# A planner that prices the SBUF port shared by VectorE and GpSimd, and rope additions with an operand in PSUM

## The chip, the core and the metric

One core of a Trainium2 chip runs the whole program. The metric is the device time of one execution in microseconds; the time of a kernel is the median of its runs.

Five engines work side by side, each through its own instructions in their written order: TensorE (PE, matrix products, weight loads shown apart as PEld), VectorE (DVE), ScalarE (ACT), GpSimd (POOL), and SyncE (SP), which issues most DMAs. They meet through semaphores.

## The reference: two layers of a hybrid decoder

The inputs are a prompt of 512 tokens and 8 samples of 4 tokens with a past of 2048. Each of two layers computes

```
h = rmsnorm(x) * norm_w;  z = h @ w_in          # 1024 -> 3584 columns
rq, rk, rv, rg, mq, mk, mv, mg, pu, pg = split(z)
rq = rope(heads(rq)); rk = rope(heads(rk)) / 8
mq = rope(rmsnorm(heads(mq), q_norm_w)); mk = rope(rmsnorm(heads(mk), k_norm_w))
mix = concat(retention(rq, rk, rv) * silu(rg),
             block_sparse_attention(mq, mk, mv) * silu(mg),
             causal_pooling(pu) * silu(pg))
x = x + mix @ w_out
```

with 6 heads of 64 in retention and in attention. The rope of a head of 64 is `x * C + swap(x) * S`, where C and S hold cosines and sines, with the norm weights multiplied in for mq and mk, and swap exchanges the halves of 32. The samples attend to a paged cache of 2048 keys, of which the best three blocks of 256 and the own tokens count. Outputs are x, the new keys and values, and the states of retention and pooling. All of it is in float32.

## The kernel before

**Dense products.** Tokens are tiles of 128 (t = 0 to 3 of the prompt; t = 4 is the 32 sample rows). A weight chunk of 384 or 256 columns comes as four slices (`wraw`, in layer 0's first chunk `pk`). A slice is split into a rounded high part, cast by ACT, and a low part `whl = wraw - high`, a subtraction that DVE or POOL does (`low`, in `split_weights`). The activations are split in the same way into `XT`. Three passes of PE over the high and low parts then stand for one float32 product. The accumulators are two PSUM banks, `acc`: a prompt tile takes 8 x 3 = 24 matmuls of PE, and the bank is free again when the last reader of the tile is done with it.

**What follows a product.** `projected` (L616) does the rope of the q and k tiles. It multiplies the accumulator by C into an SBUF buffer `t1`, the swapped halves by S into a second one `t2` (both shown as `t`), and frees `acc`. For mq and mk it sums the squares, which ACT wrote, into `qst`; POOL takes the power -1/2 of them in `rsq`; and DVE adds `t1 + t2` and multiplies by the result into `qk` (the sample keys into `ks`). For rq and rk nothing comes from POOL, and the addition may go to DVE or POOL. PE then transposes the tile (`tr<-cst,qk`). `post_gate` multiplies a silu gate `t` into `mix` (DVE or POOL), and `split_mix` splits `mix` into `XT` (the low part on DVE or POOL). `norm_tokens` at the start squares x (ACT or POOL) and adds the squares up (DVE or POOL) in `qT` and `kT`. `pool` sums the pooling windows on POOL alone (`tabs`, `s`).

**Who goes where, and in what order.** Nothing of this order is written by hand. The code is a set of generators that yield what they want next: an engine (`R("DVE")`) or a choice of engines (`R("DVE|POOL")`), flags to wait for, buffers to take. `_Plan.run` keeps a clock for each engine and starts the task that can start first; the time that it adds for each instruction is the estimate in `_Timed`'s `call`. `_Plan._start` picks the engine of a choice: the one whose start is earliest, where POOL's start counts 0.7 us later than it is. Instructions are emitted in the planned order, so this clock settles the order on each engine; what happens on the chip is then governed by semaphores.

Dense products have the lowest priority on PE. The 16 units of sample attention in each layer (`dec`, `pv`) fill in, as their pages (`pk`, `pv_`) land.

Of the kernel before, what the change touches and what calls it, by code (L numbers as in the profile page):

```python
# [24 lines left out]
H = 6  # L25
# [92 lines left out]
class _Plan:  # L118
# [7 lines left out]
    HOLD = 0.6  # L126
    SWITCH = 0.1

    def __init__(self):
        self.mode = FULL  # L130
        self.fill = False
        self.free = {e: 0.0 for e in ("PE", "ACT", "DVE", "POOL", "SP")}
        self.dma_free = 0.0
        self.done = {}
        self.res = {k: [0.0] * n for k, n in RES.items()}
        self.tasks = []
        self.seq = 0
        self.now = 0.0
        self.engine = None
        self.stage = 0  # L140
        self.dur = 0.0
        self.late = []

    def spawn(self, gen, prio=5, at=None):
        self.seq += 1
# [34 lines left out]
    def _start(self, t):  # L180
        engines, keys, get, mode = t["want"]
        at = t["ready"]
        if engines == t.get("engine"):
            at -= self.HOP[engines]
        for k in keys:
            if k not in self.done:
                return None
            at = max(at, self.done[k])
        for name in set(get):
            n = get.count(name)  # L190
            r = self.res[name]
            if len(r) < n:
                return None
            at = max(at, sorted(r)[n - 1])
        best = None
        for e in engines.split("|"):
            s = max(at, self.free[e])
            if e == "SP":
                s = max(s, self.dma_free - 3.0)
            c = s + (0.7 if e == "POOL" and "|" in engines else 0.0)  # L200
            if e == "PE" and t["prio"][0] < 9:
                late = self.MARGIN
                if mode != self.mode:
                    late = self.HOLD if self.mode == FULL else 0.3
                c = max(at + late, self.free[e])
            if best is None or c < best[0]:
                best = (c, s, e)
        c, s, e = best
        return c if e == "PE" else s, s, e
# [33 lines left out]
def R(engines, keys=(), get=(), mode=FULL):  # L243
    return engines, tuple(keys), tuple(get), mode


class _Timed:
# [10 lines left out]
    def __getattr__(self, op):  # L258
        f = getattr(self.eng, op)

        def call(*args, **kw):
            aps = [x for x in list(args) + list(kw.values()) if hasattr(x, "free_size")]
            n = max(x.free_size() for x in aps)
            psum = any(x.space == PSUM for x in aps)
            if self.name == "DVE":
                points = sum(1 for x in args[2:] if hasattr(x, "free_size"))
                fast = op in ("tensor_copy", "tensor_scalar", "memset") and not psum
                us = ((n / 2 if fast else n) + 66) / 960.0 + 0.065 * points
            elif self.name == "ACT":
                more = sum(1 for k in ("bias", "scale", "accum_out") if hasattr(kw.get(k), "free_size"))  # L270
                more += op == "mul"
                us = n / 1200.0 + (0.05 if psum else 0.093) + 0.093 * more
            elif op == "memset":
                us = 0.03 + n * 0.00085
            elif kw.get("op") == OP.pow:
                us = 0.3 + n * 0.165
            else:
                us = 0.153 + n * 0.0021

            spans = [self._span(x) for x in aps]  # L280
            if self.last and self.last[0] == self.plan.stage and any(
                    t == self.last[1] and lo <= self.last[3] and self.last[2] <= hi for t, lo, hi in spans):
                us += 0.127
            out = kw["out"] if "out" in kw else args[0]
            self.last = (self.plan.stage,) + self._span(out)
            self.plan.use(self.name, us)
            return f(*args, **kw)  # L287

        return call
# [3 lines left out]
def trunk(ctx, tc, depth, xp, xt, xs, xst, kv, sret, spool, pt, nrow, ncol, lpar, w384, w256, cst, y0,  # L293
# [14 lines left out]
    def buf(tag):  # L308

        if tag == "whl":  # L310
            return sb([128, 2, 768], tag, RES[tag], dt=F32R)
        if tag in ("vst", "kst", "oPT"):
            return sb([96, SHAPES[tag]], tag, RES[tag], dt=F32R)
        return sb([128, SHAPES[tag]], tag, RES[tag])
# [50 lines left out]
    def heads(x):  # L365
        return x.rearrange("p (h e) -> p h e", h=H)
# [249 lines left out]
    def projected(a, dst, t, Ct, St, scale=None, eps=None, norm=None):  # L616


        rows = 128 if t < 4 else NS
        src = a[:, :384]  # L620
        if t == 4:
            yield from join_sample(a, dst[:NS], 384, norm)
            src = dst[:NS]
        s3, d3 = heads(src), heads(dst[:rows])
        if scale is None:
            if t == 4:
                yield R("ACT", (), ["t1"])
                sq = buf("t1")
                A.activation(heads(sq[:rows]), s3, AF.Square)
            else:  # L630
                yield R("ACT")
                sq = dst
                A.activation(d3, s3, AF.Square)
        yield R("DVE", (), ["t1", "t2"])
        t1, t2 = heads(buf("t1")[:rows]), heads(buf("t2")[:rows])
        V.tensor_tensor(out=t1, in0=s3, in1=Ct[:rows][:, None, :].to_broadcast([rows, H, HD]), op=OP.mult)
        sa = St[:rows, 0:32][:, None, :].to_broadcast([rows, H, 32])
        sb_ = St[:rows, 32:64][:, None, :].to_broadcast([rows, H, 32])
        V.tensor_tensor(out=t2[:, :, 0:32], in0=s3[:, :, 32:64], in1=sa, op=OP.mult)
        V.tensor_tensor(out=t2[:, :, 32:64], in0=s3[:, :, 0:32], in1=sb_, op=OP.mult)  # L640
        if t < 4:
            X.put("acc")
        if scale is None:
            st = sb([128, 2, 8], "qst", 2)
            V.tensor_reduce(out=st[:rows, 0, :H], in_=heads(sq[:rows]), axis=AX, op=OP.add)
            if t == 4:
                X.put("t1")
            yield R("POOL")
            rsq(st[:rows, 1, :H], st[:rows, 0, :H], H, rows, 1.0 / HD, EPS if eps is None else eps)
            scale = st[:rows, 1, :H]  # L650
            yield R("DVE")
            V.tensor_tensor(out=t1, in0=t1, in1=t2, op=OP.add)
        else:
            yield R("DVE|POOL")
            add2(d3 if scale is False else t1, t1, t2, OP.add)
            if scale is not False:
                yield R("DVE")
        if scale is not False:
            V.tensor_tensor(out=d3, in0=t1, in1=scale[:, :, None].to_broadcast([rows, H, HD]), op=OP.mult)
        X.put("t1")  # L660
        X.put("t2")

    def stacked(src, dst, low):

# [1206 lines left out]
```

## Time and profile before

| | us |
|---|---|
| median of 3 runs (lowest, highest) | 710.14 (709.77, 712.19) |
| the profiled execution: its time | 708.43 |
| its span, first to last instruction | 706.3 |

| engine | busy us | share |
|---|---|---|
| PE | 680.0 | 96% |
| DVE | 491.5 | 70% |
| ACT | 331.4 | 47% |
| POOL | 147.4 | 21% |

Matmuls overlap, and their ends are modelled, so PE's 96% is not a measure of how well it is used. What counts is where PE stood idle, and for whom. A row such as `PE tr L335 <- DVE qk` says that PE's transposes waited for a DVE instruction that writes `qk`. Almost every vector instruction is recorded on one line (L287, the helper that calls it), so its tiles name it: `whl<-wraw,whl` is the low part of a weight slice. A duration in a timeline row is that of all its instructions together, from the first start to the last end.

### The profile page before, as it was taken

Reading aid. Unit: us, or ns where it says so; the run is one execution under the profiler, and the core shown is the slowest. Engines: PE = TensorE matmul, PEld = TensorE weight load, DVE = VectorE, ACT = ScalarE, POOL = GpSimd, SP = SyncE. Lnnn points to the kernel's source line nnn. Section 1 sums busy time; section 2 is a strip of 40 time slices with the busy share of each in tenths; the row PEclk is TensorE's granted clock in tenths of the full one; section 3 lists DMA queues with packets and bytes.
Section 4 is the critical chain, followed back from the end, with each engine's and each line's share of the span. In section 5 each row is a group of like instructions: output and inputs, shape, how many; then the busy total and the mean of one; then the engine's idle time right before and its main releaser. Section 6 shows DMA issues by size and latency. Waiting matters only on the chain.

```text
span 706.3 us, 16977 instructions
## 1 busy us (share of the span) xinstructions
PE 680.0 (96%) x5940; PEld 572.4 (81%) x5940; DVE 491.5 (70%) x1130; ACT 331.4 (47%) x839; POOL 147.4 (21%) x165
## 2 busy tenths in 40 slices
PE   6999999999999999989999999999999999999998
PEld 4887777778878878889989767777787778889898
DVE  6868898788655469876385588986855546887632
ACT  6444667654322415355264336766624233347511
POOL 7333332200101004321141223330100010045000
PEclk9999999999999999999999999999999999999999
DMA  8467889696899894406655679899999987110552
GB/s 318 179 224 248 290 266 316 213 331 216 252 304 322 255 326 160 130 12 205 225 148 168 209 247 325 281 317 287 288 336 295 319 286 224 38 62 3 168 177 78
DMA packets 111366, 159.76 MB, mean 226 GB/s; under 512 B 13937, under 2 KB 96114, under 8 KB 111282
## 3 DMA queue, kind: packets, MB, share of 16 engines
q1 hardware_dynamic: 111010, 158.43, 68.7%
q8 instruction: 47, 0.77, 0.4%
q10 hardware_dynamic: 272, 0.26, 0.1%
q14 instruction: 37, 0.30, 0.1%
HBM read 148.80 MB, written 9.84 MB: 225 GB/s over the span
## 4 chain that ended last, share of the span: by engine, by line
PE 79%; DVE 12%; ACT 2%; issue 2%; DMA 2%; POOL 1%; SPq 1%; DVEq 0%; POOLq 0%; ACTq 0%
PE acc L325 50%; PE dec L325 10%; PE pv L325 10%; PE tr L335 6%; PE att L325 3%; DVE whl L287 2%; DVE qk L287 2%; DVE t L287 1%; DVE XT L287 1%; DMA wraw<-w 1%; DMA mix<-xt 1%; DVE mix L287 1%; SPq L1638 1%; ACT whl L287 1%; DVE pt L287 1%
## 5 line engine op out<-in xcount | busy, mean ns | idle before, releaser
L325 PE MATMUL acc<-whl,XT 128*128 128x384 f32 (+1 forms) x1680 | 313.2, 339 | 8.2 <-ACT whl L287 3.0
L325 PEld LDWEIGHTS acc<-whl,XT 128*128 128x128 f32 x1680 | 282.6, 190 | 26.1 <-issue 12.5
L325 PE MATMUL acc<-XT,whl 128*128 128x256 f32 (+1 forms) x960 | 139.5, 296 | 1.0 <-DVE t L287 1.0
L325 PEld LDWEIGHTS acc<-XT,whl 128*128 128x128 f32 x960 | 125.0, 190 | 8.8 <-issue 6.3
L287 ACT CAST whl<-wraw 128x768 fp32r<-128x768 f32 (+1 forms) x100 | 76.9, 781 | 40.7 <-PE acc L325 30.2
L287 DVE TENSOR_TENSOR whl<-wraw,whl 128x768 fp32r<-128x768 f32 (+1 forms) x79 | 74.1, 947 | 28.8 <-ACT whl L287 27.5
L287 POOL TENSOR_TENSOR whl<-wraw,whl 128x768 fp32r<-128x768 f32 (+1 forms) x21 | 36.8, 1752 | 123.3 <-ACT whl L287 123.3
L325 PE MATMUL dec<-pk,qblk 128*32 128x256 f32 x768 | 50.3, 383 | 0.9 <-PE acc L325 0.6
L325 PEld LDWEIGHTS dec<-pk,qblk 128*32 128x32 f32 x768 | 24.1, 109 | 18.5 <-issue 5.8
L287 DVE TENSOR_TENSOR pv<-pv,cst 128x384 f32<-128x384 f32 x40 | 22.5, 563 | 19.5 <-PE pv L325 19.2
L287 ACT ACTIVATE dP<-dec,stat 128x256 f32<-128x256 f32 x32 | 15.2, 474 | 36.4 <-DVE stat L287 36.2
L287 ACT ACTIVATE P<-att,ast 128x128 f32<-128x128 f32 (+3 forms) x48 | 25.2, 530 | 10.7 <-DVE ast L287 8.8
L287 POOL TENSOR_TENSOR mix<-mix,t 128x256 f32<-128x256 f32 x8 | 6.4, 799 | 110.7 <-DVE t L287 83.8
L287 DVE TENSOR_TENSOR mix<-acc,qk 128x384 f32<-128x384 f32 (+1 forms) x24 | 12.2, 509 | 22.5 <-PE acc L325 22.1
L287 POOL TENSOR_TENSOR qst<-qst,mhalf 128x6 f32<-128x6 f32 (+1 forms) x20 | 26.7, 1336 | 1.7
L287 DVE TENSOR_TENSOR t<-acc,cst 128x192 f32<-128x192 f32 (+1 forms) x48 | 17.3, 417 | 10.9 <-PE acc L325 10.8
L287 ACT COPY PT<-tr 128x128 f32<-128x128 f32 (+3 forms) x41 | 16.4, 422 | 17.3 <-PE tr L335 17.2
L287 ACT ACTIVATE t<-acc 128x256 f32<-128x256 f32 (+1 forms) x32 | 12.6, 394 | 22.0 <-DVE acc L287 11.2
L287 DVE TENSOR_REDUCE stat<-dec 128x1 f32<-128x256 f32 x32 | 13.4, 419 | 13.4 <-PE dec L325 13.2
L287 ACT ACTIVATE dPT<-dec 128x256 f32<-128x256 f32 x32 | 12.2, 381 | 21.1 <-PE pv L325 21.1
L335 PE MATMUL tr<-cst,qk 128*128 128x128 f32 (+1 forms) x108 | 18.0, 275 | 3.8 <-DVE qk L287 3.6
L335 PE MATMUL tr<-cst,P 128*128 128x128 f32 x120 | 20.0, 281 | 1.5 <-DVE P L287 0.7
(503 smaller groups left out, 1211.6 us busy)
## 6 DMA issues: line engine op xcount, KB each, us to landing
pk<-kv SPq DMA_DIRECT2D x256, 192.0 KB, 3.9
wraw<-w SPq DMA_DIRECT2D x76, 384.0 KB, 4.6
wraw<-w SPq DMA_DIRECT2D x24, 256.0 KB, 4.1
y<-mix SPq DMA_DIRECT2D x4, 512.0 KB, 3.5
mix<-xt SPq DMA_DIRECT2D x7, 256.0 KB, 6.3
pk<-w SPq DMA_DIRECT2D x4, 384.0 KB, 5.1
o_vp<-tv SPq DMA_DIRECT2D x8, 192.0 KB, 1.9
o_kp<-qk SPq DMA_DIRECT2D x8, 192.0 KB, 4.3
```

Of the source, the lines that this page charges most:

```text
L287: return f(*args, **kw)
L325: nc.tensor.matmul(out, lhsT, rhs, start=start, stop=stop)
L335: nc.tensor.transpose(out, in_, ident[:n, :n])
L1638: S.dma_start(mix[:, 2 * kp:2 * kp + 2, 256 * h:256 * h + 256], col3_(xt[h, kp]))
```

## The change

Three things change.

1. The planner's clock knows of a port. A DVE instruction of 64 or more columns without an operand in PSUM, and with two tensors or a form that runs at double rate, may not overlap with a POOL instruction of 64 or more columns other than a power. Whichever is planned second gets the remaining time of the other added to its own.
2. Where DVE and POOL may be chosen, POOL counts as starting 3.0 us later (`POOL_LAST`), not 0.7.
3. In `projected` the product with C is written back in place, into the accumulator (for t = 4 into SBUF, as its source is there). The addition reads the accumulator and `t2`, always runs on DVE, and stands right behind the sum of squares. The accumulator is freed after the addition, not before it. The power on POOL is a task of its own, and only the last multiplication waits for it. The buffer `t1` is no longer used for it.

```diff
+    POOL_LAST = 3.0
...
-            c = s + (0.7 if e == "POOL" and "|" in engines else 0.0)
+            c = s + (self.POOL_LAST if e == "POOL" and "|" in engines else 0.0)
...
+            t = self.plan.now + self.plan.dur
+            port = self.plan.port
+            if self.name == "DVE" and not psum and n >= 64 and (
+                    points >= 2 or fast or op in ("tensor_tensor", "scalar_tensor_tensor")):
+                lo, hi = port["POOL"]
+                if lo < t + us and hi > t:
+                    us += hi - max(lo, t)
+                port["DVE"] = t + us
+            elif self.name == "POOL" and kw.get("op") != OP.pow and n >= 64:
+                if port["DVE"] > t:
+                    us += port["DVE"] - t
+                port["POOL"] = t, t + us
...
-        V.tensor_tensor(out=t1, in0=s3, in1=Ct[:rows][:, None, :].to_broadcast([rows, H, HD]), op=OP.mult)
...
         V.tensor_tensor(out=t2[:, :, 32:64], in0=s3[:, :, 0:32], in1=sb_, op=OP.mult)
-        if t < 4:
-            X.put("acc")
+
+        V.tensor_tensor(out=s3, in0=s3, in1=Ct[:rows][:, None, :].to_broadcast([rows, H, HD]), op=OP.mult)
         if scale is None:
...
-            yield R("POOL")
-            rsq(st[:rows, 1, :H], st[:rows, 0, :H], H, rows, 1.0 / HD, EPS if eps is None else eps)
+            key = ("qn", X.stage)
+
+            def root():
+                yield R("POOL")
+                rsq(st[:rows, 1, :H], st[:rows, 0, :H], H, rows, 1.0 / HD, EPS if eps is None else eps)
+                X.flag(*key)
+
+            X.spawn(root(), 1, X.then())
             scale = st[:rows, 1, :H]
-            yield R("DVE")
-            V.tensor_tensor(out=t1, in0=t1, in1=t2, op=OP.add)
+            V.tensor_tensor(out=d3, in0=s3, in1=t2, op=OP.add)
+            if t < 4:
+                X.put("acc")
+            X.put("t2")
+            yield R("DVE", [key])
         else:
-            yield R("DVE|POOL")
-            add2(d3 if scale is False else t1, t1, t2, OP.add)
...
+            V.tensor_tensor(out=d3, in0=s3, in1=t2, op=OP.add)
+            if t < 4:
+                X.put("acc")
+            X.put("t2")
         if scale is not False:
-            V.tensor_tensor(out=d3, in0=t1, in1=scale[:, :, None].to_broadcast([rows, H, HD]), op=OP.mult)
+            V.tensor_tensor(out=d3, in0=d3, in1=scale[:, :, None].to_broadcast([rows, H, HD]), op=OP.mult)
```

What it does to the instructions, counted over the whole order: POOL has 41 wide instructions that the planner could have put elsewhere before, and 12 now. The weight slices on POOL go from 21 to 9, the gates from 8 to 0, the parts of `XT` from 7 to 2, the sums of the first norm from 4 to 1, the rope additions from 1 to 0. The 12 window sums stay. DVE takes 12 weight slices, 8 gates, 5 parts of `XT` and one sum of the norm more; ACT takes two squares of the norm. PE runs the same matmuls in another interleaving.

At the start, POOL's first wide instructions before are the squares of x (`qT<-mix`), sums of them (`qT<-qT`) and a weight slice; `rs` is the norm itself:

```order
L287 TENSOR_TENSOR qT<-mix 128x1024 x2
L287 TENSOR_TENSOR qT<-qT 128x1024
L287 TENSOR_TENSOR qT<-qT 128x512
L287 TENSOR_TENSOR whl<-wraw,whl 128x768
L287 TENSOR_TENSOR rs<-rs,mhalf 128x2
```

and now:

```order
L304 TENSOR_TENSOR qT<-qT 128x1024
L304 TENSOR_TENSOR whl<-wraw,whl 128x768
L304 TENSOR_TENSOR rs<-rs,mhalf 128x1
L304 TENSOR_SCALAR rs<-rs 128x1
L304 TENSOR_TENSOR rs<-rs,mhalf 128x2
```

The two squares and one sum have left POOL.

On DVE, one prompt tile of mk in layer 0 before, from the rope's products to the multiplication by the power (`qst`); `pv`, `att` and their results are other tasks' work between:

```order
L287 TENSOR_TENSOR t_1188<-acc,tabs 128x384
L287 TENSOR_TENSOR t_1189<-acc,tabs 128x6x32 x2
L287 TENSOR_REDUCE qst<-qk 128x6
L287 COPY kTs<-tr 128x96
L287 TENSOR_TENSOR pv<-pv,cst 128x384
L287 TENSOR_REDUCE On<-pv 128x64
L287 TENSOR_TENSOR att<-att,cst 128x2x128
L287 TENSOR_REDUCE ast<-att 128x2
L287 TENSOR_TENSOR t_1188<-t_1188,t_1189 128x384
L287 TENSOR_TENSOR qk<-t_1188,qst 128x384
```

and a tile of the same chunk now:

```order
L304 TENSOR_TENSOR t_1049<-acc,tabs 128x6x32 x2
L304 TENSOR_TENSOR acc<-acc,tabs 128x384
L304 TENSOR_REDUCE qst<-qk 128x6
L304 TENSOR_TENSOR qk<-acc,t_1049 128x384
L304 TENSOR_TENSOR pv<-pv,cst 128x384
L304 TENSOR_REDUCE On<-pv 128x64
L304 TENSOR_TENSOR klz<-tr,kT 64x3x128 x2
L304 TENSOR_TENSOR qk<-qk,qst 128x384
```

The addition, which reads `acc` now, stands right behind the sum of squares. Before it stood behind the other tasks' work, and `acc` was free before them, after the products.

On POOL, between the powers of the mk tiles of layer 0 (`qst`) and the weight slices of the next chunk, before:

```order
L287 TENSOR_SCALAR qst<-qst,rs 32x6
L287 TENSOR_TENSOR qst<-qst,mhalf 32x6
L287 TENSOR_TENSOR whl<-wraw,whl 128x512 x2
L287 TENSOR_SCALAR qst<-qst,rs 128x6
L287 TENSOR_TENSOR qst<-qst,mhalf 128x6
L287 TENSOR_TENSOR whl<-wraw,whl 128x512
```

and now:

```order
L304 TENSOR_SCALAR qst<-qst,rs 32x6
L304 TENSOR_TENSOR qst<-qst,mhalf 32x6
L304 TENSOR_SCALAR qst<-qst,rs 128x6
L304 TENSOR_TENSOR qst<-qst,mhalf 128x6
L304 TENSOR_SCALAR qst<-qst,rs 128x6
L304 TENSOR_TENSOR qst<-qst,mhalf 128x6
L304 TENSOR_TENSOR whl<-wraw,whl 128x512
```

Two of the three slices have gone to DVE.

## Rows read from the trace of the kernel before

**Rows 1.** The page: span, and busy time of each engine (share of span, instructions).

```profile
span 706.3 us, 16977 instructions
PE 680.0 (96%) x5940; PEld 572.4 (81%) x5940; DVE 491.5 (70%) x1130; ACT 331.4 (47%) x839; POOL 147.4 (21%) x165
```

**Rows 2.** The page: share of the span on the chain that ended last.

```profile
PE 79%; DVE 12%; ACT 2%; issue 2%; DMA 2%; POOL 1%; SPq 1%; DVEq 0%; POOLq 0%; ACTq 0%
```

**Rows 3.** Waits of PE: line, released by, total us, times, longest.

```profile
PE tr L335 <- DVE qk L287: 3.6, 4, 1.2
...
PE acc L325 <- DVE XT L287: 2.3, 1, 2.3
...
PE acc L325 <- DVE mix L287: 2.1, 1, 2.1
...
PE dec L325 <- DVE mixs L287: 1.1, 1, 1.1
...
PE acc L325 <- DVE t L287: 1.0, 1, 1.0
```

**Rows 4.** Timeline, layer 1, last key tile: start, us, engine, instruction [idle before].

```profile
620.38 0.55 DVE L287 TENSOR_TENSOR t<-t,t 128x384 f32<-128x384 f32 x1
...
620.96 1.81 POOL L287 TENSOR_TENSOR whl<-wraw,whl 128x768 fp32r<-128x768 f32 x1
...
620.97 2.21 DVE L287 TENSOR_TENSOR qk<-t,cst 128x384 f32<-128x384 f32 x1
...
623.24 0.55 PE L335 MATMUL tr<-cst,qk 128*128 128x128 f32 x3 [1.24 <-DVE qk L287]
```

**Rows 5.** Timeline, layer 0, VectorE and GpSimd side by side.

```profile
54.62 1.09 DVE L287 TENSOR_TENSOR t<-acc,tabs 128x384 f32<-128x384 f32 x3
...
54.79 1.84 POOL L287 TENSOR_TENSOR whl<-wraw,whl 128x768 fp32r<-128x768 f32 x1 [5.61 <-ACT whl L287]
```

**Rows 6.** Timeline, layer 0: a GpSimd power beside VectorE adds.

```profile
295.35 1.33 POOL L287 TENSOR_TENSOR gst<-gst,mhalf 128x6 f32<-128x6 f32 x1
...
295.67 1.01 DVE L287 TENSOR_TENSOR XT<-mix,XT 128x384 fp32r<-128x384 f32 x2
```

**Rows 7.** Groups by form: PE, VectorE, GpSimd: xcount | busy us, mean ns | idle before.

```profile
L325 PE MATMUL acc<-whl,XT 128*128 128x384 f32 x1488 | 289.7, 346 | 8.2 <-ACT whl L287 3.0 <-DVE XT L287 2.3 <-DVE mix L287 2.1
...
L287 DVE TENSOR_TENSOR whl<-wraw,whl 128x768 fp32r<-128x768 f32 x60 | 61.1, 1030 | 21.8 <-ACT whl L287 20.5 <-DMA wraw<-w 0.4
...
L287 DVE TENSOR_TENSOR mix<-mix,t 128x256 f32<-128x256 f32 x24 | 12.0, 500 | 0.5
...
L287 DVE TENSOR_TENSOR t<-t,t 128x384 f32<-128x384 f32 x23 | 13.7, 594 | 0.3
...
L287 DVE TENSOR_TENSOR t<-acc,cst 128x384 f32<-128x384 f32 x16 | 8.9, 556 | 10.9 <-PE acc L325 10.8
...
L287 DVE TENSOR_REDUCE qst<-qk 128x6 f32<-128x384 f32 x16 | 8.7, 542 | 0.0
...
L287 POOL TENSOR_TENSOR whl<-wraw,whl 128x768 fp32r<-128x768 f32 x16 | 30.4, 1900 | 120.6 <-ACT whl L287 120.6
...
L287 POOL TENSOR_TENSOR qst<-qst,mhalf 128x6 f32<-128x6 f32 x16 | 21.4, 1340 | 1.3
```

**Rows 8.** Timeline of the start: GpSimd sums, VectorE, PE.

```profile
11.16 5.73 DVE L287 TENSOR_TENSOR whl<-pk,whl 128x768 fp32r<-128x768 f32 x2
...
13.07 4.94 POOL L287 TENSOR_TENSOR qT<-qT 128x1024 f32<-128x1024 f32 x2
...
16.81 1.87 DVE L287 SCALAR_TENSOR_TENSOR XT<-mix,ncol,XT 128x256 fp32r<-128x256 f32 x2
...
18.34 0.97 PE L325 MATMUL acc<-whl,XT 128*128 128x384 f32 x4 [2.30 <-DVE XT L287]
```

**Rows 9.** Waits of PE's weight loads, same columns as rows 3.

```profile
PEld acc L325 <- DVE t L287: 2.5, 6, 1.2
```

**Rows 10.** Windows: stretch, us; busy us (count) of PE, PEld, DVE, ACT, POOL; PEclk, DMA, GB/s.

```profile
40.00:100.00 60.00, 58.10 (x480) 48.01 (x478) 50.32 (x109) 31.56 (x86) 20.56 (x22) 0.97 0.80 255
```

More of the change, by code (lines that the diff above doesn't have):

```diff
@@ L142, in __init__ @@
         self.late = []
+        self.port = {"DVE": 0.0, "POOL": (0.0, 0.0)}
     def spawn(self, gen, prio=5, at=None):
@@ L633, in projected @@
                 A.activation(d3, s3, AF.Square)
-        yield R("DVE", (), ["t1", "t2"])
-        t1, t2 = heads(buf("t1")[:rows]), heads(buf("t2")[:rows])
-        V.tensor_tensor(out=t1, in0=s3, in1=Ct[:rows][:, None, :].to_broadcast([rows, H, HD]), op=OP.mult)
+        yield R("DVE", (), ["t2"])
+        t2 = heads(buf("t2")[:rows])
         sa = St[:rows, 0:32][:, None, :].to_broadcast([rows, H, 32])
@@ L647, in projected @@
                 X.put("t1")
-            yield R("POOL")
-            rsq(st[:rows, 1, :H], st[:rows, 0, :H], H, rows, 1.0 / HD, EPS if eps is None else eps)
-            scale = st[:rows, 1, :H]
-            yield R("DVE")
-            V.tensor_tensor(out=t1, in0=t1, in1=t2, op=OP.add)
-        else:
-            yield R("DVE|POOL")
-            add2(d3 if scale is False else t1, t1, t2, OP.add)
-            if scale is not False:
-                yield R("DVE")
+            key = ("qn", X.stage)
[4 more added lines that the diff above has]
+            X.spawn(root(), 1, X.then())
+            scale = st[:rows, 1, :H]
+            V.tensor_tensor(out=d3, in0=s3, in1=t2, op=OP.add)
[3 more added lines that the diff above has]
+            yield R("DVE", [key])
+        else:
+            V.tensor_tensor(out=d3, in0=s3, in1=t2, op=OP.add)
+            if t < 4:
+                X.put("acc")
+            X.put("t2")
         if scale is not False:
-            V.tensor_tensor(out=d3, in0=t1, in1=scale[:, :, None].to_broadcast([rows, H, HD]), op=OP.mult)
-        X.put("t1")
-        X.put("t2")
+            V.tensor_tensor(out=d3, in0=d3, in1=scale[:, :, None].to_broadcast([rows, H, HD]), op=OP.mult)
     def stacked(src, dst, low):
```

## The prediction

> **What bounds the kernel now.** I read the page first, then the chain that ended last, then PE's waits by releaser, and last the timeline at the longest of these waits. PE is busy in 680.0 of the span's 706.3 us, so only some 26 us are open idle time [rows 1]. Matmuls overlap: the widest group has a mean of 346 ns each, but 289.7 us for 1488 is one per 195 ns [rows 7]. So an idle row of PE begins only after a modelled end, and each stall is about 0.15 us longer than its row. PE holds 79% of the chain that ended last and DVE 12%; POOL has 1% [rows 2]. A change that touches DVE and POOL alone can therefore gain only where PE waited for DVE, and those places can be listed: PE's transposes for `qk`, its products for `XT`, `mix` and `t`, the sample products for `mixs`, together 3.6 + 2.3 + 2.1 + 1.0 + 1.1 = 10.1 us in 8 waits [rows 3]. With 0.15 us for each they are 11.3 us.
>
> What made DVE late there is to be seen in layer 1's last key tile. The addition of 384 columns took 0.55 us. The multiplication of the same width right behind it took 2.21 us, since POOL's weight slice began 0.01 us ahead of it and took 1.81; DVE ended 0.41 us after POOL, as if it had started when POOL stopped. PE's transposes stood idle 1.24 us for it [rows 4]. Against this stands a tile where DVE reads the accumulator: three products took 1.09 us although a slice on POOL lay over most of them [rows 5]. So it is not POOL as such, it is two SBUF operands against POOL's. The start shows the same: two weight slices on DVE took 5.73 us, while a slice has a mean of 1.03 [rows 7]; POOL was adding up squares from 13.07 to 18.01; two `XT` parts then took 1.87, and PE stood idle 2.30 us [rows 8].
>
> The Trainium skill says in "SBUF — State Buffer", section "Who interferes with whom", that the port pair that the two engines share is an exclusive lock, and that an instruction which gets it first keeps it to its end. The slices in rows 4 agree. The powers do not: a power on POOL ran from 295.35 for 1.33 us, and two additions of 384 columns on DVE started inside it and took 1.01 together, no more than alone [rows 6]. The planner leaves powers out of its port times. By the page that is an error of up to 1.34 us for each of the 16 powers of the norms [rows 7], 21 us that the clock would not see, and then the change would gain nothing; by the rows it costs nothing, and I go by the rows. A result of no change from this cause has no chance of its own here.
>
> **The change part by part.** The sum is made against the profiled execution, 708.43 us with 706.3 of span. The median of the runs shown is 710.14, 1.7 higher, and 1.7 is added at the end.
>
> *Fewer and later collisions.* By the order, POOL's movable wide instructions go from 41 to 12; with the 12 window sums, which stay, 24 of 53 are left, and the clock now keeps these away from DVE's where it can. In addition the rope's addition, which was a victim, reads PSUM and can't be one any more. The bounds are nothing and all of the 11.3 us. I take three quarters, 8.5, because more than half of the colliders are gone, and the rest are planned apart, but by a clock of estimates, which the chip need not follow. At the start three of POOL's four sums and squares leave it, so the 2.30 us should go nearly whole. What is late next there is ACT, which has to make two of the squares between its casts of the slices.
>
> *The addition on the accumulator.* A rope product from PSUM of 384 columns has a mean of 556 ns, the addition from SBUF 594 with its collisions and 0.55 without [rows 4, 7]. So 32 prompt tiles pay nothing for the PSUM operand itself (32 x 0.006 = 0.2 us at most on DVE, which is 70% busy). The product in place writes PSUM; I price it like one that only reads it, and no row speaks of more.
>
> *The power beside the addition.* Before, a q or k tile waited for POOL's power (1.34 us [rows 7]) and then made the addition and the multiplication. Now the addition lies beside the power. At the four waits for `qk` of rows 3 this is worth 0.55 each at most, 2.2 us; at least nothing, since these tiles were late by collisions that I have already taken away. I take nothing.
>
> *The accumulator is held longer.* It was free after the products; now the sum of squares (0.54 [rows 7]) and the addition (0.56) come first in the 16 normalised prompt tiles, 1.10 us, and the addition alone in the 16 of rq and rk. PE makes a tile in 24 x 0.195 = 4.7 us and has a second bank. From the end of a tile, ACT's square, DVE's products at 1.09 [rows 5] and now 1.10 more fit into that, unless DVE is backed up. Six weight loads waited for such a release before, 2.5 us together [rows 9]. If each of them waits 1.10 longer, that is 6.6 us; at the other end it is nothing, where PE finds a unit of sample attention to do. The planner sees the later release and reorders for it. I take 1.5, near the low end, since the six waits have 0.4 us each, which says that the bank comes late by little and seldom.
>
> *More work on DVE.* 12 weight slices at 1.03 at most, 8 gates at 0.50, 5 parts of `XT` at about 0.6 (like the additions of 384 columns) and a sum of about 1 are 12.4 + 4.0 + 3.0 + 1.0 = 20.4 us [rows 7]. Behind each of them are queued the other tiles' products and sums, for which PE waits. On the other side DVE loses the stretches, of which the start alone has 5.73 - 2.06 = 3.7 us, and every collision like that of rows 4 a further 1.66. The bounds are a gain (DVE ends with less busy time than before) and 20.4 us, if all lay on PE's path. I weigh it by DVE's share of the chain, 12%: 2.4 us. The cover is that DVE is idle in 30% of the span; it is thin from 40 to 100 us, where DVE is busy 50.3 of 60 [rows 10].
>
> Sum: 708.4 - 8.5 + 1.5 + 2.4 = 703.8, and with 1.7 to the median 705.5. I say **705 us**.
>
> **The rivals.** *Slower: the accumulators become the bound.* Where DVE is backed up, the later release lands on PE. All tiles together hold their bank 16 x 1.10 + 16 x 0.56 = 26.6 us longer. If half of it is on PE's path, 13.3 us, the sum is 708.4 - 8.5 + 13.3 + 2.4 + 1.7 = 717. It decides from the point where PE's waits for a release grow by more than about 6 us, which eats the rest of the gain. For it speak DVE's 84% in rows 10 and that the stage can't be interrupted; against it that PE has two banks and other work, and rows 9.
>
> *No change: the clock doesn't keep them apart.* In the new order a slice on POOL still stands behind the first group norm's powers in layer 1, the place of rows 4. If the chip drifts off the plan, what is left collides as before and only the removed instructions count: 4 us instead of 8.5 gives 708.4 - 4.0 + 1.5 + 2.4 + 1.7 = 710.0. The same comes out if DVE, which has to make four slices at a chunk's start in 4.1 us while PE takes 4.7 for a tile, makes PE wait 0.25 us at each of 26 chunks: 6.5 in place of the 2.4 and 1.5 above gives 708.
>
> *More than forecast.* All 11.3 us go, PE finds work during the later releases, DVE gets quicker on balance, and the norm at the start comes earlier, by what DVE was stretched there beyond PE's own wait, 3.7 - 2.3 = 1.4 us: 708.4 - 11.3 - 1.4 + 1.7 = 697.
>
> **How the numbers follow.** Within 0.3% of 710.14 is 708.0 to 712.3, about what a measurement of this kernel can tell from no change. The forecast as worked out, 700 to 708, has 0.43; more than that 0.17; no change 0.18; slower 0.22, of which half is the accumulators and half the plain chance that the new interleaving on PE meets new waits, since the whole order of 706 us is dealt again. So faster has 0.43 + 0.17 = 0.60. The range reaches into both sides, 695 to 714; the forecast's own is 700 to 708.
>
> **What would show it.** Right: the DVE forms with two SBUF tensors have nearly one duration, so wide slices fall from a mean of 1030 to below 1000 ns; PE's waits for `qk` and `XT` fall from 5.9 to under 2 us; POOL is some 30 us less busy (nine wide slices at 1.90 are 17 of it), and DVE between 480 and 500. PE's first accumulators of the second chunk start some 2 us earlier. Wrong: waits of PE's weight loads for a DVE instruction that reads `acc` (now named `qk`) of more than 8 us; waits for `whl` on DVE that weren't there; or collisions that remain, with the same multiplications of 384 columns at over 1.5 us.

## The result and the profile after

The changed kernel takes 699.38 us (median of 4 runs, 698.75 to 699.74). Beside it the kernel before took 709.95 (4 runs, 706.79 to 712.19). The ratio is 0.9853, with a 95% interval of 0.9815 to 0.9892: faster by 10.6 us, where 5 were forecast. The profiled execution took 698.75 us.

The page of the changed kernel, the same rows as in [rows 1, 2]:

```profile
span 697.0 us, 16955 instructions
...
PE 676.4 (97%) x5940; PEld 568.5 (82%) x5940; DVE 489.4 (70%) x1169; ACT 330.6 (47%) x831; POOL 106.8 (15%) x134
...
PE 86%; DVE 8%; ACT 2%; issue 2%; DMA 1%; POOL 0%; DVEq 0%; ACTq 0%
```

The span is 9.3 us shorter. POOL is 40.6 us less busy; DVE, which got the work, is busy 2.1 us less than before; its share of the chain fell from 12% to 8%.

DVE's groups by form after the change (xcount | busy us, mean ns), to set beside [rows 7]:

```profile
L304 DVE TENSOR_TENSOR whl<-wraw,whl 128x768 fp32r<-128x768 f32 x69 | 67.5, 989 | 13.2 <-ACT whl L304 12.6
...
L304 DVE TENSOR_TENSOR qk<-acc,t 128x384 f32<-128x384 f32 x32 | 17.8, 557 | 1.1
...
L304 DVE TENSOR_TENSOR mix<-mix,t 128x256 f32<-128x256 f32 x32 | 13.4, 419 | 0.3
...
L304 DVE TENSOR_TENSOR acc<-acc,cst 128x384 f32<-128x384 f32 x16 | 9.1, 566 | 0.6
...
L304 DVE TENSOR_TENSOR qk<-qk,qst 128x384 f32<-128x384 f32 x16 | 8.9, 554 | 1.7 <-POOL qst L304 1.5
```

Nine more weight slices of 768 columns and eight more gates, yet the mean slice fell from 1030 to 989 ns and the gate from 500 to 419. The addition that reads `acc` costs 557 ns, and the product written back into `acc` 566, where the product into SBUF had 556.

PE's waits by releaser after the change (total us, times, longest), beside [rows 3]:

```profile
PE acc L342 <- ACT whl L304: 3.2, 1, 3.2
PE tr L352 <- DVE XT L304: 2.6, 3, 1.2
PE acc L342 <- DVE t L304: 2.4, 2, 1.8
...
PE acc L342 <- DVE mix L304: 1.3, 1, 1.3
PE acc L342 <- DVE qk L304: 1.1, 1, 1.1
...
PE tr L352 <- DVE qk L304: 0.8, 1, 0.8
PE dec L342 <- DVE mixs L304: 0.8, 1, 0.8
```

The transposes for `qk` went from 3.6 us in four waits to 0.8 in one, and the 2.30 us for `XT` at the start is gone. Waits for `t` (from 1.0) and for transposes of `XT` (from 1.4) grew; not every new row is good.

Layer 1's last key tile in the timeline after the change (start, us), the place of [rows 4]:

```profile
616.10 0.56 DVE L304 TENSOR_TENSOR qk<-acc,t 128x384 f32<-128x384 f32 x1
...
616.69 0.56 DVE L304 TENSOR_TENSOR qk<-qk,cst 128x384 f32<-128x384 f32 x1
616.92 2.02 POOL L304 TENSOR_TENSOR whl<-wraw,whl 128x768 fp32r<-128x768 f32 x1 [3.86 <-ACT whl L304]
```

The multiplication takes 0.56 us in place of 2.21. POOL's slice still comes, but behind its start, and now POOL is the longer one.

**What I had not looked at: TensorE's clock.** The mean granted clock of the profiled execution was 0.995 before and 1.000 after. Windows of the kernel before (columns as in [rows 10]), each time the stretch ahead of a fall of the clock and the stretch at the low level:

```profile
85.50:89.10 3.60, 2.32 (x38) 1.88 (x39) 3.53 (x12) 1.81 (x6) 1.07 (x2) 1.00 0.90 266
89.10:92.50 3.40, 3.40 (x19) 2.85 (x17) 3.23 (x7) 1.21 (x6) 1.78 (x2) 0.50 0.99 324
...
307.40:311.00 3.60, 1.46 (x9) 1.14 (x8) 3.53 (x11) 2.55 (x8) 0.00 (x0) 1.00 0.00 0
311.00:314.40 3.40, 3.40 (x12) 3.33 (x11) 0.30 (x2) 0.93 (x2) 0.00 (x0) 0.50 0.18 58
```

In the first place PE had stood idle for `t`, in the second for `mix`: two of the eight waits of [rows 3]. Behind each of them PE ran 3.40 us at 0.50, which is 1.2 of 2.4 GHz. Where PE sets the pace, that costs another 1.7 us. So the 2.1 us for `mix` had a price of nearly 4. The same two places after the change:

```profile
85.60:89.20 3.60, 2.26 (x17) 1.91 (x16) 3.50 (x10) 0.27 (x1) 1.53 (x2) 1.00 0.94 302
89.20:92.60 3.40, 3.40 (x29) 3.06 (x28) 2.45 (x9) 1.47 (x7) 0.07 (x1) 1.00 1.01 309
300.00:303.60 3.60, 2.17 (x12) 1.54 (x10) 3.60 (x10) 3.15 (x10) 0.00 (x0) 1.00 0.00 0
303.60:307.00 3.40, 3.40 (x37) 2.95 (x41) 2.76 (x7) 1.24 (x2) 0.00 (x0) 1.00 0.16 58
```

PE waited there too, 1.1 and 1.3 us, and the clock stayed at 1.00. The length of a wait alone does not tell: the clock fell behind 1.0 us for `t` before, and it did not fall behind the 2.30 us of [rows 8], nor behind the longest wait for `t` after the change, 1.8 us. The Trainium skill says in "TensorE: Matmul & The Clock Gate", section "What's actually happening", that an idle array falls to 1.2 GHz and that work brings it back. The rows of before agree; those of after show that a wait of this size need not do it.

From every run's mean clock I work out what it gave up, as (1 - clock) x span: a stretch of T at half clock lowers the mean by T/2 of the span, and PE, where it is busy all the time, loses T/2. The median is 5.0 us over 51 runs of the kernel before, and 1.7 over the 4 of the changed kernel. The pages of the two profiled executions agree: for the same 5940 matmuls PE is busy 680.0 us before and 676.4 after, 3.6 us less, and the two low stretches of 3.40 us come to 3.4.

### The profile page after: what moved, and what is told of

Read it like the earlier page. It is cut to its first block, busy times and chain, and to the rows that moved or that the text cites. A ratio compares the mean times of both kernels' runs of the same rounds, so it can differ in the third digit from the quotient of the medians.

```text
span 697.0 us, 16955 instructions
## 1 busy us (share of the span) xinstructions
PE 676.4 (97%) x5940; PEld 568.5 (82%) x5940; DVE 489.4 (70%) x1169; ACT 330.6 (47%) x831; POOL 106.8 (15%) x134
## 4 chain that ended last, share of the span: by engine, by line
PE 86%; DVE 8%; ACT 2%; issue 2%; DMA 1%; POOL 0%; DVEq 0%; ACTq 0%
PE acc L342 54%; PE pv L342 12%; PE dec L342 10%; PE tr L352 6%; PE att L342 4%; DVE whl L304 2%; DVE XT L304 1%; DMA mix<-xt 1%; ACT whl L304 1%; DVE t L304 1%; DVE acc L304 1%; DVE qk L304 0%; ACT kT L304 0%; DVE kT L304 0%; DMA pk<-kv 0%
## 5 line engine op out<-in xcount | busy, mean ns | idle before, releaser
L304 DVE TENSOR_TENSOR whl<-wraw,whl 128x768 fp32r<-128x768 f32 (+1 forms) x91 | 83.3, 928 | 16.6 <-ACT whl L304 16.0
L342 PE MATMUL dec<-pk,qblk 128*32 128x256 f32 x768 | 48.3, 383 | 0.0
L342 PEld LDWEIGHTS dec<-pk,qblk 128*32 128x32 f32 x768 | 21.8, 109 | 17.4 <-issue 4.3
L304 DVE TENSOR_TENSOR mix<-acc,qk 128x384 f32<-128x384 f32 (+1 forms) x24 | 12.2, 508 | 24.7 <-PE acc L342 23.8
L304 POOL TENSOR_TENSOR whl<-wraw,whl 128x768 fp32r<-128x768 f32 (+1 forms) x9 | 17.7, 1971 | 53.7 <-issue 28.5
L304 DVE TENSOR_REDUCE stat<-dec 128x1 f32<-128x256 f32 x32 | 13.5, 421 | 15.4 <-PE dec L342 15.1
L304 ACT ACTIVATE dPT<-dec 128x256 f32<-128x256 f32 x32 | 12.2, 382 | 24.8 <-PE pv L342 24.7
L304 ACT ACTIVATE dP<-dec,stat 128x256 f32<-128x256 f32 x32 | 15.1, 473 | 15.8 <-DVE stat L304 15.7
L304 ACT ACTIVATE t<-acc 128x256 f32<-128x256 f32 (+1 forms) x32 | 12.6, 394 | 18.9 <-PE acc L342 10.2
L304 DVE TENSOR_REDUCE ast<-att 128x2 f32<-128x256 f32 (+3 forms) x24 | 19.8, 825 | 0.8
L304 ACT ACTIVATE PT<-PT,gst 128x64 f32<-128x64 f32 x48 | 16.8, 428 | 6.6 <-POOL gst L304 6.6
```

What stands on the lines that cost most here:

```text
L342: nc.tensor.matmul(out, lhsT, rhs, start=start, stop=stop)
```

## The experiments

The theory was that VectorE's collisions with GpSimd's wide instructions make PE wait. The rivals were that the planner's port clock, the operand in PSUM or plainly another deal of the order makes the difference. (In the expectations theory 1 is the collisions, rival 2 the deal, rival 3 the rope's form.) Two numbers of each run's profile tell them apart. *Stretched* is, summed over DVE's instructions that lie beside a POOL instruction of 64 columns or more, their duration less the median of the same form undisturbed (a form that is never undisturbed doesn't count); in brackets the part behind 30 us. *Clock* is the loss as above, a median over the runs, and *rest* the median of the times less their own clock loss. All ratios are to the kernel before, run beside them; each median is of 4 to 12 runs. The kernel before took 709.95 to 711.45 us in the four sets of runs, so medians of different sets compare to about 1 us.

| run | median us | ratio (95%) | stretched us | clock us | rest us |
|---|---|---|---|---|---|
| before, 51 runs | 710.93 | | 31.7 (29.0) | 5.0 | 705.7 |
| the change | 699.38 | 0.9853 (0.9815, 0.9892) | 13.0 (10.8) | 1.7 | 697.9 |
| e1_nocollide | 696.75 | 0.980 (0.9784, 0.9817) | 12.5 (6.0) | 1.4 | 695.4 |
| e2_last | 708.36 | 0.9966 (0.9944, 0.9988) | 17.9 (15.7) | 7.1 | 701.2 |
| e3_port | 714.15 | 1.0061 (1.004, 1.0081) | 29.0 (17.5) | 10.7 | 703.7 |
| e4_rope | 707.34 | 0.995 (0.993, 0.997) | 21.2 (17.9) | 4.2 | 702.9 |
| e5_last_port | 710.01 | 0.9987 (0.9961, 1.0013) | 18.7 (16.6) | 5.3 | 704.4 |
| e6_last_rope | 701.28 | 0.9861 (0.9838, 0.9884) | 12.2 (10.1) | 4.9 | 696.4 |
| e7_port_rope | 706.94 | 0.9932 (0.9909, 0.9956) | 38.2 (25.0) | 3.5 | 702.5 |
| e8_never | 701.80 | 0.9867 (0.9836, 0.9899) | 4.4 (4.4) | 7.3 | 694.6 |
| e9_jitter_before | 716.37 | 1.0074 (1.0047, 1.0101) | 23.0 (20.0) | 10.7 | 706.6 |
| e10_jitter_after | 706.72 | 0.9941 (0.9919, 0.9962) | 12.4 (10.2) | 6.3 | 700.6 |
| e11_sbuf_add | 701.95 | 0.9873 (0.985, 0.9896) | 14.9 (12.8) | 2.8 | 698.9 |
| e12_nocollide_after | 694.47 | 0.9774 (0.975, 0.9798) | 4.7 (2.5) | 1.4 | 693.1 |

**e1, the order of before without its collisions.** All engines but POOL have the order of the kernel before. POOL's movable wide instructions after 40 us are replaced by narrow powers of like duration and a memset or an instruction of 8 columns; that computation is left out.

```diff
     def add2(out, in0, in1, op):
+        if X.engine == "POOL" and X.now > 40:
+            n = out.free_size()
+            low = out.dtype == F32R and op == OP.subtract and n in (512, 768) and len(out.ap) == 2
+            k = {768: 5, 512: 3}[n] if low else {384: 3, 256: 2}.get(n, 0)
+            if k:
+                nc.gpsimd.tensor_tensor(out=filler[:, :k], in0=ones[:, :k], in1=mhalf[:, :k], op=OP.pow)
+            if low:
+                X.use("POOL", 0.153 + n * 0.0021)
+                nc.gpsimd.memset(out.bitcast(F32), 0.0)
+                return
...
```

> The kernel before with its order unchanged on PE, DVE, ACT and SP. From 40 us on, POOL's movable wide instructions no longer read SBUF widely: a weight slice's low part is set to zero (a memset) behind a power of a few columns, gates and XT parts treat 8 columns, also behind a power, so that POOL is busy about as long (768 columns: power of 5 columns and memset, some 1.87 us for 1.84). It leaves out that part of the computation. Theory 1 (collisions on the shared port are what the change removed): the waits of PE for qk, mix, mixs and t that follow stretched DVE instructions go, 6 to 8 us; 702 to 704 us, and DVE's wide slices all near 0.95 us. Rival 2 (the gain is the new interleaving, whatever it is made by): the order is the old one, so 708 to 711. Rival 3 (the rope's form gains it): also 708 to 711.

It took 696.75 us, 2.0% less than before and 5 us below the 702 to 704 that theory 1 gave, with POOL as busy as before (150.4 us). The place of [rows 4] in its timeline (POOL's `filler` is the power, DVE's two instructions are the same as there):

```profile
610.69 0.55 DVE L287 TENSOR_TENSOR t<-t,t 128x384 f32<-128x384 f32 x1
...
611.27 1.18 POOL L347 TENSOR_TENSOR filler<-ones,mhalf 128x5 f32<-128x5 f32 x1
...
611.28 0.59 DVE L287 TENSOR_TENSOR qk<-t,cst 128x384 f32<-128x384 f32 x1
```

The multiplication of 2.21 us took 0.59 beside a power of 1.18. So it was POOL's wide reads and not its being busy. (A memset of 0.74 us also ends a weight slice on POOL sooner than a subtraction of 1.84; but in the kernel before no wait of PE is for a slice from POOL.) With the order held fixed, 19.2 us less of stretch (23.0 less behind 30 us) made the time 13.6 us shorter than that of before in its set (710.37): 3.6 by the clock and 10.0 by the rest. Windows of this run at the two times at which the clock had been low:

```profile
89.10:92.50 3.40, 3.40 (x41) 2.48 (x42) 3.32 (x11) 2.28 (x8) 1.41 (x2) 1.00 1.03 372
...
311.00:314.40 3.40, 3.40 (x35) 2.99 (x28) 1.93 (x4) 1.03 (x2) 0.00 (x0) 1.00 0.65 181
```

The clock is at 1.00 in both; this run has one low stretch, in the first 30 us, where the collisions were left in. With the collisions both falls are gone.

**e2 to e7, the three parts alone and in pairs.** e2 has only the later start of POOL, e3 only the port clock, e4 only the rope edit; e5 to e7 are the pairs. The edits are those of the change, so a line or two stand for each; the rope edit is the third part of the diff.

```diff
# e2, e5, e6 (in e3, e4, e7 it is 0.7)
+    POOL_LAST = 3.0
...
# e3, e5, e7
+                if lo < t + us and hi > t:
+                    us += hi - max(lo, t)
...
# e4, e6, e7
+            V.tensor_tensor(out=d3, in0=s3, in1=t2, op=OP.add)
...
```

> The kernel before with POOL's start counted 3.0 us later, nothing else. POOL makes 13 weight slices for 21, no gates. Theory 1: fewer collisions, about half of the gain: 703 to 706. Rival 2: any time between 700 and 715, with no relation to the stretched DVE time. Rival 3: 709 to 711.

> The kernel before with the clock that knows the port, nothing else. POOL makes 20 weight slices, so as many as before, but planned apart from DVE's two-operand work. Theory 1: half or more of the gain, 702 to 706, with stretched DVE time falling from 31.7 us to under 15. If the clock does not follow the chip, 708 to 711 with the stretches still there. Rival 2: any time between 700 and 715. Rival 3: 709 to 711.

> The kernel before with the rope edit alone (product in place in PSUM, addition from PSUM on DVE behind the sum of squares, power beside it, accumulator freed after the addition). Theory 1: the additions no longer collide, 1 to 3 us: 707 to 709. Rival 3 (the rope's form gains most of it): 700 to 704. If the longer held accumulator costs, 712 to 716.

> The planner's two parts without the rope edit: port clock and POOL's start 3.0 us later. Theory 1 (what counts is the stretched DVE time): 13 weight slices on POOL and rope additions from SBUF; stretched time near the 17.9 us of the 3.0 us alone, so 703 to 707, 3 to 7 us slower than the whole change. Rival 2 (each edit deals the order anew, and the time is luck): anywhere from 700 to 715. Rival 3 (the rope edit is worth what it gave alone, 3 us): 702.

> POOL's start 3.0 us later and the rope edit, without the port clock. 8 weight slices on POOL. Theory 1: few collisions are left without any clock for the port, stretched time about 10 to 13 us, 699 to 703. If the clock is what tells them apart: 705 to 708. Rival 2: anywhere from 700 to 715.

> Port clock and rope edit, POOL's start 0.7 us later as before. 29 weight slices on POOL, more than before. Theory 1: pricing a collision does not avoid it, stretched time 20 to 30 us, 706 to 714. If the clock and the rope carry the gain: 699 to 703. Rival 2: anywhere.

The times that theory 1 gave came for e4, e6 and e7; e2, e3 and e5 are 2.4, 8.2 and 3.0 us slower than the upper ends of theirs. The port clock alone made the kernel slower (1.0061), and the two other parts without it are as fast as the whole change: 0.9861 against 0.9853, within both intervals. Alone it left 29.0 us of stretch and 43 movable wide instructions on POOL (41 before). Behind 30 us it did cut the stretch, from 29.0 to 17.5 us, but beside the other parts it cut nothing: 16.6 us in e5 against 15.7 in e2, 25.0 in e7 against 17.9 in e4, 10.8 in the change against 10.1 in e6. Why pricing a collision doesn't avoid it I have not tried; the price falls on whichever is planned second, and the start of neither is moved by it. In e3 PE stood idle at 86 us, and the clock fell for long; its windows:

```profile
86.10:89.70 3.60, 0.76 (x5) 0.53 (x5) 3.44 (x10) 2.38 (x10) 1.04 (x1) 1.00 0.97 335
89.70:99.90 10.20, 8.23 (x61) 6.11 (x59) 6.80 (x23) 4.34 (x19) 3.17 (x4) 0.51 0.82 279
```

The stretch of 10.20 us at the low level costs up to 5.1. By the rest e3 is faster than before by 2.0 us; the granted clock takes 5.7 more.

Neither the later start of POOL (0.9966) nor the rope edit (0.995) brings much alone. Together they bring more than their sum (0.9861), and this holds with the clock taken out: 705.7 to 701.2, 702.9 and 696.4. What they bring beyond their sum there, 2.0 us, is no more than single orders scatter by (1.9, below). The pair e7 has the most stretch of all, 38.2 us, and is still faster than before: 13.2 us of it lie in the first 30 us, where the rest of the time does not follow (below).

**e8, the choice never falls on POOL.**

```diff
-    POOL_LAST = 3.0
+    POOL_LAST = 1000.0
```

> The whole change, but POOL's start counted 1000 us later, so that POOL makes nothing that DVE can make, only powers and the window sums. Theory 1: hardly any collision is left (window sums), stretched time under 8 us; DVE has 9 wide slices more. If collisions are all, 695 to 699; if DVE's own load then counts, 700 to 705. Rival 2: anywhere from 700 to 715.

It has 4.4 us of stretch, 8.6 less than the change, and is no faster: 0.9867 (0.9836, 0.9899), in the range expected if DVE's own load counts. Its rest is 694.6, 3.3 us below that of the change, but the clock gives up 7.3 where the change gives up 1.7. That does not clear DVE: PE's longest waits for `t`, `qk` and `mix` from DVE are 2.4, 2.2 and 1.8 us, where the change had 1.8, 1.1 and 1.3, and the clock falls at waits for DVE (1.0 us for `row`, 1.5 for `P`, the 1.8 for `mix`). Whether DVE's larger load made them, or the deal, is not shown.

**e9 and e10, the order dealt anew.** One number of the planner that belongs to no part of the change, in the kernel before (e9) and in the changed one (e10).

```diff
-    HOP = {"PE": 0.2, "ACT": 0.2, "DVE": 0.18, "POOL": 0.2, "SP": 0.12}
+    HOP = {"PE": 0.2, "ACT": 0.2, "DVE": 0.20, "POOL": 0.2, "SP": 0.12}
```

> The kernel before, with one number of the planner changed that belongs to neither part of the change: the delay it counts from an end on VectorE to a start elsewhere, 0.20 in place of 0.18 us. All instructions and their arithmetic stay, but the order is dealt anew (28 wide whl subtractions and 16 other wide instructions on GpSimd, against 21 and 20). Collision theory: about as many collisions, 28 to 36 us of stretched VectorE time, so within 0.5% of before, 707 to 714 us. Luck-of-the-deal rival (any new order is worth as much as the change was): as far away as the change took it, under 703 or over 717 us, with the stretched time no guide to it.

> The changed kernel with the same number changed, 0.20 in place of 0.18 us (10 wide whl subtractions and 2 other wide instructions left on GpSimd, against 9 and 3). Collision theory: 10 to 16 us of stretched VectorE time and a ratio to before of 0.982 to 0.989, 698 to 703 us. Luck-of-the-deal rival: back to 705 us or more.

Both expectations of the collision theory failed: 716.37 and 706.72 us, 5.4 and 7.3 more than their twins, at less stretch or the same. The rival had e10 right (705 or more), and e9 came between the two. The deal of the order is worth as much as most parts of the change. Most of it is the clock: 10.7 and 6.3 us given up, against 5.0 and 1.7, so 5.7 and 4.6 more. Windows of e10 around two of its four low stretches:

```profile
85.80:89.40 3.60, 2.00 (x15) 1.69 (x16) 3.50 (x9) 0.28 (x1) 1.43 (x2) 1.00 0.99 306
89.40:92.80 3.40, 3.40 (x17) 3.39 (x16) 0.99 (x5) 0.40 (x1) 0.17 (x1) 0.50 0.99 348
362.30:365.90 3.60, 1.91 (x23) 1.49 (x25) 3.57 (x7) 2.84 (x9) 2.09 (x4) 1.00 0.71 203
365.90:369.30 3.40, 3.40 (x36) 2.34 (x26) 3.40 (x4) 0.75 (x2) 1.47 (x1) 0.50 0.55 187
```

In the first, PE waited 1.6 us for the addition that reads `acc`, where it had waited 1.1 in the change; half a microsecond more, and the clock fell; but 1.0 us had been enough in the kernel before, so what decides it stays open. The longest wait of e10 is 4.5 us for a gate's `t` at 280 us, with no wide instruction of POOL near it, so it is no collision there. But the step from one deal to the other is the same: 716.37 to 706.72 is 9.65 us, 709.95 to 699.38 is 10.6. So in both deals the change itself is worth some 10 us, and the rival that all of it was luck falls, as far as two deals can say.

**e11, the addition from SBUF.** Only the operand is undone; the early addition and the power beside it stay.

```diff
-        V.tensor_tensor(out=s3, in0=s3, in1=Ct[:rows][:, None, :].to_broadcast([rows, H, HD]), op=OP.mult)
+        V.tensor_tensor(out=t1, in0=s3, in1=Ct[:rows][:, None, :].to_broadcast([rows, H, HD]), op=OP.mult)
+        if t < 4:
+            X.put("acc")
...
-            V.tensor_tensor(out=d3, in0=s3, in1=t2, op=OP.add)
+            V.tensor_tensor(out=d3, in0=t1, in1=t2, op=OP.add)
```

> The changed kernel with one thing of the rope edit undone: the product with the cosines goes into the SBUF buffer t1 again and the accumulator is given back after the products, so that the addition has no operand in PSUM. That the addition stands ahead of GpSimd's power, which runs beside it, and the new planner rules stay. If the operand in PSUM is what the rope edit is worth (one more SBUF-only VectorE instruction per tile that can collide, 16 of 384 columns in each of two layers): 704 to 707 us. If the edit works by the order it gives (the addition no longer waits for the power, the whole chain of one head block runs through): 697 to 702 us, with at most 2 us of collisions on the additions.

701.95 us, 0.9873 with an interval that overlaps the change's: the operand in PSUM is not shown to be worth anything, and giving the accumulator back early, as e11 does, makes nothing faster. The stretch is 1.9 us more, the rest 1.0. What the rope edit brings beside POOL's later start (e5, without it, took 710.01) may then be mostly its order, the addition ahead of the power; as a new deal moves the time by nearly as much, this is not shown.

**e12, the changed order without the collisions that are left.** The edit of e1 in the changed kernel, the order on all engines but POOL kept; ten wide instructions of POOL are replaced, that computation is left out.

```diff
+        if X.engine == "POOL" and X.now > 40:
+            G.alt = narrow
         {"POOL": G, "DVE": V}[X.engine].tensor_tensor(out=out, in0=in0, in1=in1, op=op)
```

> The changed kernel with its order on TensorE, VectorE, ScalarE and SyncE unchanged; the wide instructions that the planner may move and had left on GpSimd after 40 us (9 in all) are replaced there by narrow powers of like duration and a memset or an 8-column instruction, so that computation is left out. What the collisions still cost in the changed kernel: 13.0 us of stretched VectorE time should fall to 4 to 8. If stretched time still counts as it did before the change (19 us less of it made 13.6 us there): 692 to 696 us. If what is left lies off the path, or VectorE's own work is the next bound (which the run without any movable work on GpSimd points to): 698 to 700.5 us.

694.47 us, 4.9 less than the change, for 8.3 us less of stretch and nearly the same clock. So what was left after the change lay on the path still, at 0.58 us for each (4.8 us by the rest).

Over all fourteen kernels the rest follows the stretch behind 30 us: a least-squares fit on both parts of the stretch gives 693.3 us plus 0.53 for each us behind 30 us, with 1.9 us of scatter, and -0.12 for the first 30 us; with DVE's busy time less the stretch as a third term, that term has -0.03 with a standard error of 0.15. The medians don't line up so well: the clock adds between 1.4 and 10.7 us to them. Of the kernels that compute everything none is faster than the changed one.

## Why the prediction was right in sign and short in size

**Collisions, -8.5: the mechanism right, the size too small.** Behind 30 us the stretch fell from 29.0 to 10.8. At 0.43 (e1, 10.0 for 23.0) to 0.58 (e12, 4.8 by the rest for 8.3) for each of these 18.2 us, that is 7.9 to 10.6 us. The start, 2.3 of the 8.5, comes on top. Windows of the first 30 us, before and after, then of the rest of the span: before, after, e1, e12 (columns as in [rows 10]):

```profile
0.00:30.00 30.00, 21.83 (x110) 19.25 (x111) 24.69 (x37) 16.94 (x29) 18.04 (x19) 1.00 0.75 273
0.00:30.00 30.00, 25.19 (x150) 22.72 (x151) 21.31 (x38) 18.65 (x31) 12.24 (x17) 1.00 0.78 276
...
30.00:706.30 676.30, 658.18 (x5832) 553.15 (x5830) 466.84 (x1094) 314.47 (x810) 129.41 (x147) 0.99 0.69 224
30.00:697.00 667.00, 651.24 (x5792) 545.81 (x5790) 468.13 (x1132) 311.91 (x800) 94.56 (x117) 1.00 0.70 227
30.00:693.50 663.50, 654.77 (x5835) 551.86 (x5833) 445.37 (x1094) 314.37 (x810) 133.16 (x183) 1.00 0.71 229
30.00:691.00 661.00, 650.01 (x5787) 546.39 (x5785) 458.96 (x1130) 312.12 (x799) 93.87 (x127) 1.00 0.72 229
```

In the first 30 us PE is idle 8.2 us before and 4.8 after, 3.4 less. All eight kernels with POOL's later start have 4.7 to 5.3 there, the six others 6.4 to 8.7. Whether fewer collisions make this or the squares that moved to ACT is not shown; the stretch counted there is 2.7 us before and 2.2 after. If all of the start were theirs, the collisions would make 11.3 to 14.0. Behind 30 us PE's idle time fell from 18.1 to 8.7 in e1 and from 15.8 to 11.0 in e12, where the order was held, but only from 18.1 to 15.8 in the change itself.

**The clock: a term that the sum lacked.** It is worth 3.3 us (5.0 to 1.7). The row was there: PEclk 0.97 over 60 us in [rows 10] is 1.8 us given up, and I read from it only DVE's busy time. The step that failed is "each stall is about 0.15 us longer than its row": a stall behind which the clock fell cost 1.7 more, and two of the eight waits of [rows 3] had one. It is this term that took the time out of the range of 700 to 708: with 3.6 us more of busy PE the profiled execution of the changed kernel would have had 702.4, where 703.8 was forecast.

**What kept them apart: the step failed.** I put the port clock beside the smaller number of instructions as a cause. e3, e5 and e6 show no gain from the port clock; POOL's later start and the rope edit do it. The rival "the clock doesn't keep them apart" was right in its premise and wrong in its price: it counted what then remains as 4 us, while the two other parts alone bring 9.9 (0.0139 of 711).

**The power beside the addition, 0, and the accumulator, +1.5.** They can't be told apart by these runs, but the wait that I feared is not there. Waits of PE's weight loads for DVE's readers of `acc` after the change (columns as in [rows 9]):

```profile
PEld acc L342 <- DVE t L304: 2.1, 1, 2.1
PEld acc L342 <- DVE mix L304: 1.6, 1, 1.6
PEld acc L342 <- DVE qk L304: 1.3, 1, 1.3
```

The addition that now frees the bank is the reader named `qk`: one wait of 1.3 us, where 8 would have decided for the slower rival. The row of [rows 9] was read too wide: of its six waits three, 1.65 us, are for the rope's products, and three, 0.82, for the gates, which read `acc` into `t` too; the 2.1 after the change is for a gate. e11, which holds the bank no longer than the kernel before, is no faster.

**More work on DVE, +2.4.** DVE's work beside the stretch rose from 459.8 to 476.4 us (489.4 - 13.0). What that cost is known only as a remainder: behind 30 us 7.9 to 10.6 us of collisions went, by the prices of e1 and e12, and PE's idle time fell by 2.4. So by this estimate the moved work, the accumulators and the deal gave 5.5 to 8.2 us back, where I had 3.9 for the first two. Which of them it was stays open. The fit gives the moved work no weight, but the kernels that have it also have the quicker start, which the fit doesn't know, and the deal alone moved the rest by 0.9 and 2.7 us in e9 and e10.

So the collisions were taken too small in the sum, and so were the costs. Together I had -4.6; PE's idle time fell by 5.7 (26.3 to 20.6). That these are so near is luck. With the 3.6 us of the clock they make up the 9.3 us of span.

The list of waits that the bounds went by was short as well. The view of [rows 3] has 5.3 us more in 11 waits for DVE, the largest 1.4 for transposes of `XT`, so the 11.3 us was short as an upper bound. All waits of PE for DVE fell from 15.4 us in 19 to 10.5 in 12.

Of the signs named, the mean slice is at 989 ns (below 1000 forecast), PE's waits for `qk` and `XT` of [rows 3] at 0.8 (below 2; all its waits for these two tiles are 4.5), POOL 40.6 us less busy (30), DVE at 489.4 (480 to 500), and no 384-column multiplication is over 1.5 us: the longest took 1.31. PE starts the second chunk's dense matmuls at 29.3 us, 3.0 earlier. The time is below my forecast's own range of 700 to 708, nearest to the rival of 697, whose premises (no accumulator waits, all collisions) came in part only, with the clock in addition.

## What to carry to other kernels

Price a wait of TensorE with what its clock does behind it, and read the granted clock of each kernel before two are compared: here it hid or made up to 9 us, more than most edits. To find out what contention costs, hold the order fixed and replace the contender by an instruction of like duration that doesn't contend; leaving parts of the change out deals the order anew, which by itself moved this kernel by 5 to 7 us. And split the gain by stages before it is put down to one cause: of 5.7 us less idle time of TensorE 3.4 lay in the first 30 us.

## What was not expected of the hardware

A VectorE instruction of 8 columns took as long as the stretched multiplication of [rows 4], one of twelve of its kind. Timeline of the changed kernel, layer 1 (the DVE row holds two instructions, of which the first is the long one):

```profile
493.18 1.83 POOL L304 TENSOR_TENSOR whl<-wraw,whl 128x768 fp32r<-128x768 f32 x1 [28.50 <-issue]
493.36 2.56 DVE L304 TENSOR_SCALAR comb<-comb 128x8 f32<-128x8 f32 x2
494.95 0.74 POOL L304 MEMSET tabs<- 128x768 f32 x1
```

The longest of this kind took 2355 ns, the median is 174. It ended at 495.72, 0.03 us behind POOL's memset, so it was held through two instructions of POOL that followed each other without a gap. The Trainium skill says in "SBUF — State Buffer", section "Who interferes with whom", that instructions with a tensor and a scalar can take both ports too, and that the loser then waits for the whole instruction of the other; the row agrees, and in this one case the loser lost twice. The planner's port clock leaves out whatever has fewer than 64 columns, so it could not see this one.
